# A two-layer hybrid backbone step: first norm and first products in another order, output turned on TensorE, modulation pieces fetched two ahead

## The chip, the core and the metric

The kernel runs on one core of a Trainium2 chip. Its engines are TensorE (PE, which has a separate row for its weight loads, PEld), VectorE (DVE), ScalarE (ACT), GpSimd (POOL) and SyncE (SP). DMAs are issued by SP, ACT or POOL. The metric is the device time of one execution in microseconds; a smaller number is better. Times of runs are medians. A profile is of one execution.

## The reference

One inference step for 128 context tokens and 256 latent tokens (384 in all), model width 1024, two layers:

```python
def trunk_layer(x, cvec, lp, mix_fn):
    sh1, sc1, gt1, sh2, sc2, gt2 = adaln(cvec, lp)       # silu(c) @ w_mod + b_mod, 6 x 1024
    h = modulate(rms_norm(x, lp["norm1_g"]), sh1, sc1)   # h * (1 + scale) + shift
    qa, ka, va, u, qc, kc, vc, g = project_inputs(h, lp) # h @ w_in, q and k normed
    oa, ob, oc, aux = mix_fn(qa, ka, va, u, qc, kc, vc)  # attention, S5 scan, neighbourhood attention
    x = x + gt1[:, None, :] * merge_branches(oa, ob, oc, g, lp)
    h2 = modulate(rms_norm(x, lp["norm2_g"]), sh2, sc2)
    x = x + gt2[:, None, :] * swiglu(h2, lp)
    return x, aux
```

with `rms_norm(x, g) = x * rsqrt(mean(x*x) + 1e-6) * g`. Context tokens are modulated by `c_ctx`, latent tokens by `c`. Behind the second layer stands one more `rms_norm` with `final_g`; that is the output `y`. All is float32.

## The kernel before, in words

Activations lie transposed: `xT` holds 8 tiles of 128 features by 384 tokens. A product in float32 precision is made of three float32r matmuls: high times high, high times low, low times high. `wsplit` (line 126) loads a 512 KB weight piece through SP (`raw`), ACT casts it to the high part `hi` (line 134) and DVE subtracts for the low part `lo` (line 136). The hidden state has the same two parts, `hh` and `hl` (`shift`, line 345): ACT writes `hh`, DVE `hl`, each in two instructions, one per token group.

PE's order is the order in which the program is written. The other engines' instructions are ordered by a scheduler with priorities (`high_priority`); `issue_after` puts an instruction behind another one in that order. Every engine takes its queue in order, so an instruction that waits holds up what stands behind it.

The start of layer 0 is `first` (line 473). 28 matmuls with a zero operand (`warm`) come first. ACT squares the 8 tiles of `xT` (line 482), DVE adds them into two sums (line 484), PE sums these over features (line 325, 3 token blocks by 2 buffers), DVE takes the reciprocal root in a chain of small operations (`rsqrt`, lines 145 to 161). `mod_col` (line 421) multiplies a 1 MB piece of `w_mod` with the conditioning vector, for one tile's shift and scale together: 8 matmuls, shown in the profile as 16 records; ACT copies the result (line 434); `mod_row` (line 437) turns it into columns on PE and DVE adds the bias. `norm_bc` (line 329) broadcasts the root over partitions on PE. `first_h` scales a tile (line 455) and calls `shift`. Then, for tile d from 0 to 7, `tok_mms` (line 459) issues nine matmuls for column block 1 and nine for block 0 (line 466); between them stand the `mod_col` of tile d+2, and behind them its `mod_row`, so that PE takes the modulation in turn with the products.

`s5_lambda` prepares the constants of the S5 scan: about 90 operations on DVE of 128x32 and a little more, a sine and a cosine on ACT (lines 632 and 633), which need another activation table. Before the change, all up to its first `yield` is issued ahead of `first`, and the rest behind the products of tile 0; its results are first used by the preparation steps (`next(prep)`) behind tile 1.

Later sections of the modulation of layer 0, and of layer 1, are made in pieces of 512 KB each (`modvec`, line 222), which are taken one by one between products (`mod_steps`); each piece was loaded when its matmuls were issued to the program, with a high priority.

The end is `final` (line 1339). ACT has already scaled each tile of `xT` by its gain (`xg`, line 1335) as the last residuals come out of the feed-forward network, and `norm_sum` (line 309) has squared it and added it to one sum. PE sums over features, DVE takes the root, PE broadcasts it, DVE multiplies `xg` by it in three instructions and SP sends out each part as `yT`, still transposed.

Of the kernel before, what the change touches and what calls it, by code (L numbers as in the profile page):

```python
# [19 lines left out]
L = 2  # L20
# [21 lines left out]
N_EARLY = (11, 11)  # L42
SECTIONS = (1, 0, 2, 3, 4, 5)
# [21 lines left out]
class Net:  # L65
    def __init__(self, ctx, tc, a, o):
# [12 lines left out]
        self.mod_pending = None  # L79
        self.mrp = None  # L80
# [45 lines left out]
    def wsplit(self, src, n=1024, after=None):  # L126
# [4 lines left out]
        with self.tc.high_priority(offset=30), \  # L131
# [4 lines left out]
            nc.vector.tensor_tensor(lo[:, :n], raw[:, :n], hi.bitcast(F32)[:, :n], op=OP.subtract)  # L136
# [8 lines left out]
    def rsqrt(self, src, n, scale, eps):  # L145
        v = self.nc.vector
        x, g, w = [self.small.tile([128, 32], F32, name=f"rs_{q}", bufs=1)[:, :n] for q in "xgw"]
        yi = self.small.tile([128, 32], I32, name="rs_i")[:, :n]
        h = self.small.tile([128, 32], F32, name="rs_r")[:, :n]
        v.tensor_scalar(x, src, scale, eps, op0=OP.mult, op1=OP.add)  # L150
# [70 lines left out]

    def modvec(self, l, s, raws=None):
# [86 lines left out]
    def norm_sum(self, k):  # L309
# [4 lines left out]
        else:  # L314
            sq = self.tmp.tile([128, T], F32, name="tp")
            nc.scalar.activation(sq, self.xT[:, k, :], AF.Square)
            self.sum_last = nc.vector.tensor_tensor(self.ssq, self.ssq, sq, op=OP.add)

    def norm_rs(self):
        nc = self.nc  # L320
        ps = self.pt.tile([128, 512], F32, name="pt")
        sums = self.ssq if isinstance(self.ssq, list) else [self.ssq]
        for t in range(3):
            for i, sq in enumerate(sums):
                nc.tensor.matmul(ps[:, t:t + 1], lhsT=sq[:, t * 128:(t + 1) * 128], rhs=self.ones,
                                 start=i == 0, stop=i == len(sums) - 1)
        return self.rsqrt(ps[:, 0:3], 3, 1.0 / D, EPS)
# [93 lines left out]
    def mod_col(self, d):  # L421
        nc = self.nc
        ps = self.pt.tile([128, 512], F32, name="pt")
        with self.tc.high_priority(offset=2000):
            raw = self.qkv[:, 2048 * (d % 2):2048 * (d % 2) + 2048]
            nc.sync.dma_start(raw, self.a["wmods"][d])
# [41 lines left out]

    def load_early(self):
# [3 lines left out]
    def first(self, prep, lam):  # L473
# [1117 lines left out]
```

## Time and profile before

| | |
|---|---|
| median of 3 runs | 1273.38 us (1269.96 to 1277.38) |
| profiled execution, its own time | 1272.04 us |
| span of its trace | 1270.3 us |
| PE busy | 1235.8 us (97%) |
| PE weight loads | 1125.8 us (89%) |
| DVE busy | 884.2 us (70%) |
| ACT busy | 568.5 us (45%) |
| POOL busy | 31.0 us (2%) |
| mean DMA rate | 150 GB/s |
| mean granted TensorE clock | 0.989 |

The span is a little shorter than the execution's own time. Busy shares are means over stages with different limits, so what a change in one stage is worth is read from that stage's chain: which wait ends last there. PE is busy nearly all the time, and matmuls overlap one another in the trace: a record's duration is longer than the distance to the next one. The granted clock of TensorE has two levels, full (1.00, 2.4 GHz) and half (0.50, 1.2 GHz).

### The profile page before, as it was taken

What the parts mean: (1) busy time and instruction counts of PE and PEld (TensorE: products, weight loads), DVE (VectorE), ACT (ScalarE), POOL (GpSimd) and SP (SyncE); (2) the same over time, 40 slices, a digit from 0 to 9 for tenths busy, and PEclk for the clock granted to TensorE, in tenths of its full rate; (3) what the DMA queues carried; (4) which work ended last, traced back from release to release, by engine and by line L of the source; (5) the groups of instructions that cost most, each with busy time, mean ns of one, the idle gap of its engine ahead of it and who ended that gap; (6) DMA issues with size and microseconds to landing.
All of it is one profiled execution on the core that took longest, in us unless ns stands there. A gap on an engine that the chain in (4) does not pass through costs nothing.

```text
span 1270.3 us, 19705 instructions
## 1 busy us (share of the span) xinstructions
PE 1235.8 (97%) x7676; PEld 1125.8 (89%) x7676; DVE 884.2 (70%) x1799; ACT 568.5 (45%) x1121; POOL 31.0 (2%) x57
## 2 busy tenths in 40 slices
PE   9999999999999999999999999999999999999996
PEld 5768797887988999999997899878799999999996
DVE  7895678667778976857869886674786554555554
ACT  4373237565443433433445533755644532333442
POOL 0000000000000100000000000000000000000000
PEclk8999999999999999999999999989999999999998
DMA  8856744223656744545473332332133434334331
GB/s 313 311 198 200 249 152 132 85 78 137 209 169 217 262 160 158 174 143 170 135 269 91 121 127 93 115 105 95 56 111 106 133 117 133 119 118 133 129 102 64
DMA packets 53581, 190.16 MB, mean 150 GB/s; under 512 B 7008, under 2 KB 7056, under 8 KB 52336
## 3 DMA queue, kind: packets, MB, share of 16 engines
q1 hardware_dynamic: 46368, 167.82, 40.1%
q0 software_dynamic: 4672, 16.30, 4.0%
q10 hardware_dynamic: 2448, 4.79, 1.1%
q8 instruction: 60, 0.98, 0.3%
q14 instruction: 33, 0.27, 0.1%
HBM read 186.49 MB, written 2.39 MB: 149 GB/s over the span
## 4 chain that ended last, share of the span: by engine, by line
PE 86%; ACT 6%; DVE 4%; DMA 2%; issue 1%; SPq 0%; DVEq 0%; ACTq 0%
PE ps L141 11%; PE ps L143 11%; PE pm L141 11%; PE ps L142 11%; PE pm L142 11%; PE pm L143 11%; PE ps L466 6%; PE pm L466 3%; PE ps L236 2%; DVE lo L136 2%; ACT hi L134 1%; PE ps L1066 1%; PE ps L836 1%; PE pt L915 1%; PE pt L1132 1%; PE pt L1106 1%
## 5 line engine op out<-in xcount | busy, mean ns | idle before, releaser
L136 DVE TENSOR_TENSOR lo<-raw,hi 128x1024 fp32r<-128x1024 f32 (+1 forms) x246 | 295.1, 1200 | 174.3 <-ACT hi L134 172.9
L134 ACT CAST hi<-raw 128x1024 fp32r<-128x1024 f32 (+1 forms) x246 | 253.2, 1032 | 310.1 <-PE pm L142 108.8
L141 PE MATMUL pm<-hh,hi 128*128 128x384 f32 x550 | 191.8, 349 | 0.0
L143 PE MATMUL pm<-hh,lo 128*128 128x384 f32 x550 | 185.7, 338 | 0.0
L142 PE MATMUL pm<-hl,hi 128*128 128x384 f32 x550 | 185.4, 337 | 0.0
L143 PE MATMUL ps<-ah,lo 128*128 128x386 f32 (+1 forms) x512 | 174.1, 340 | 1.5 <-DVE lo L136 1.4
L141 PE MATMUL ps<-ah,hi 128*128 128x386 f32 (+1 forms) x512 | 174.9, 342 | 0.0
L142 PE MATMUL ps<-al,hi 128*128 128x386 f32 (+1 forms) x512 | 173.4, 339 | 0.0
L141 PEld LDWEIGHTS pm<-hh,hi 128*128 128x128 f32 x550 | 104.5, 190 | 12.9 <-issue 9.1
L141 PE MATMUL pm<-ah,hi 128*128 128x386 f32 (+1 forms) x320 | 113.1, 353 | 0.0
L143 PE MATMUL pm<-ah,lo 128*128 128x386 f32 (+1 forms) x320 | 109.1, 341 | 2.4 <-DVE lo L136 2.4
L142 PE MATMUL pm<-al,hi 128*128 128x386 f32 (+1 forms) x320 | 109.1, 341 | 0.0
L141 PE MATMUL ps<-hh,hi 128*128 128x384 f32 x314 | 105.7, 337 | 0.0
L143 PE MATMUL ps<-hh,lo 128*128 128x384 f32 x314 | 104.9, 334 | 0.0
L142 PE MATMUL ps<-hl,hi 128*128 128x384 f32 x314 | 104.9, 334 | 0.0
L142 PEld LDWEIGHTS pm<-hl,hi 128*128 128x128 f32 x550 | 104.7, 190 | 0.0
L143 PEld LDWEIGHTS pm<-hh,lo 128*128 128x128 f32 x550 | 104.2, 190 | 0.0
L143 PEld LDWEIGHTS ps<-ah,lo 128*128 128x128 f32 x512 | 96.6, 189 | 2.8 <-DVE lo L136 2.8
L141 PEld LDWEIGHTS ps<-ah,hi 128*128 128x128 f32 x512 | 96.3, 188 | 3.0 <-issue 1.9
L142 PEld LDWEIGHTS ps<-al,hi 128*128 128x128 f32 x512 | 96.8, 189 | 0.0
L141 PEld LDWEIGHTS pm<-ah,hi 128*128 128x128 f32 x320 | 60.6, 190 | 8.5 <-issue 3.4
L1224 DVE SCALAR_TENSOR_TENSOR xT<-ps,mod,xT 128x128 f32<-128x128 f32 x84 | 31.2, 412 | 51.9 <-PE ps L143 51.9
(318 smaller groups left out, 2072.1 us busy)
## 6 DMA issues: line engine op xcount, KB each, us to landing
raw<-wgu SPq DMA_DIRECT2D x88, 512.0 KB, 3.5
raw<-wg SPq DMA_DIRECT2D x48, 512.0 KB, 3.5
raw<-wq SPq DMA_DIRECT2D x28, 512.0 KB, 4.1
raw<-wd SPq DMA_DIRECT2D x32, 448.0 KB, 3.4
qkv<-wmodt POOLq DMA_DIRECT2D x24, 512.0 KB, 4.2
mr<-wmod SPq DMA_DIRECT2D x22, 512.0 KB, 4.6
qkv<-wmods SPq DMA_DIRECT2D x8, 1024.0 KB, 5.8
raw<-wo SPq DMA_DIRECT2D x16, 512.0 KB, 3.5
```

Of the source, the lines that this page charges most:

```text
L134: nc.scalar.copy(hi[:, :n], raw[:, :n])
L136: nc.vector.tensor_tensor(lo[:, :n], raw[:, :n], hi.bitcast(F32)[:, :n], op=OP.subtract)
L141: mm(ps, lhsT=wh, rhs=xh, start=start, stop=False)
L142: mm(ps, lhsT=wh, rhs=xl, start=False, stop=False)
L143: mm(ps, lhsT=wl, rhs=xh, start=False, stop=stop)
L236: nc.tensor.matmul(ps[32 * q:32 * q + cs.shape[-1], 0:256], lhsT=cs, rhs=raw[:, q * 256:(q + 1) * 256], start=k % 4 == 0, stop=k % 4 == 3)
L466: self.nc.tensor.matmul(ps[t][:, :w], lhsT=h[:, k, ts], rhs=x[:, c:c + w], start=k == 0 and i == 0, stop=k == KT - 1 and i == 2)
L836: nc.tensor.matmul(b[:, i, 0:NCOL], lhsT=G[:, 8 * d + 4 * h + i, r, :], rhs=u4[:, 4 * h + i, :], start=True, stop=True)
L915: mm(y, lhsT=E[:, 8 * d + p, r].rearrange("p a b -> p (a b)"), rhs=H[d][r][:, i, d:d + NCOL], start=False, stop=d == 1 and r == 1)
L1066: nc.tensor.matmul(u["S"][:, i, :], lhsT=Q[hb, h // 2, t * 128:(t + 1) * 128], rhs=K[hb, ks, k0:k0 + n], start=True, stop=True)
L1106: nc.tensor.transpose(pp[:, i, :], f[:, i * 128:(i + 1) * 128], self.ident)
L1224: self.res_last = self.nc.vector.scalar_tensor_tensor(self.xT[:, m, c0:c1], ps[:, c0:c1], gt[:, m, g:g + 1], self.xT[:, m, c0:c1], op0=OP. ...
```

## The change

It edits four places.

1. In `first`, the warm block has 16 matmuls instead of 28, and the block ahead of the first products 3 instead of 4. The squares go to eight buffers; tiles 5 and 7 are squared on DVE, the others on ACT. DVE adds tiles 1, 2 and 3 into tile 0; PE sums five buffers. `xT` is loaded by SP and ACT in turn, and `cT` by POOL. Tile 0 is scaled with the broadcast straight from PSUM. The first nine products are grouped by their operands. The first part of `s5_lambda` is issued behind the reciprocal root.
2. In `modvec`, pieces of layer 0 are fetched two ahead.
3. `rope` is loaded behind an output on POOL's queue, and the pieces of `mod_col` behind the weight piece last issued.
4. In `final`, PE turns `xg` back to tokens by features in 24 transposes; the last square is summed on PE without DVE's add; the root multiplies the turned tiles per token, half on ACT, half on DVE. The output `y` goes out in four DMAs.

```diff
+N_WARM = (16, 3, 3)
...
-    def rsqrt(self, src, n, scale, eps):
+    def rsqrt(self, src, scale, eps):
...
+        c = n // len(src)
+        for i, q in enumerate(src):
+            v.tensor_scalar(x[:, c * i:c * i + c], q, scale, eps, op0=OP.mult, op1=OP.add)
...
-            nc.sync.dma_start(self.cT.rearrange("p k g -> p (k g)"), a["cT"])
             self.xT = c.tile([128, KT, T], F32, name="xT")
             for k in range(0, KT, 2):
-                nc.sync.dma_start(self.xT[:, k:k + 2].rearrange("p k t -> p (k t)"),
-                                  a["xT"][:, k * T:(k + 2) * T])
+                (nc.scalar if k % 4 else nc.sync).dma_start(
+                    self.xT[:, k:k + 2].rearrange("p k t -> p (k t)"),
+                    a["xT"][:, k * T:(k + 2) * T])
+            nc.gpsimd.dma_start(self.cT.rearrange("p k g -> p (k g)"), a["cT"])
...
+    def mod_fetch(self, n):
+        while self.mod_list and len(self.mod_raws) < n:
+            self.mod_raws.append(self.mod_get(*self.mod_list.pop(0)))
...
-                with self.tc.high_priority(offset=2000):
-                    raw = self.mod_raw(l)
-                    with self.tc.issue_after(self.weights.ins):
-                        nc.sync.dma_start(raw, self.a["wmod"][l, s, k])
+                if l == 0:
+                    self.mod_fetch(2)
+                raw = self.mod_raws.pop(0) if self.mod_raws else self.mod_get(l, s, k)
...
+    def tok_first(self, ps, hi, lo):
+        for i, (h, x) in enumerate(((self.hh, hi), (self.hh, lo), (self.hl, hi))):
+            for t in range(3):
+                self.nc.tensor.matmul(ps[t], lhsT=h[:, 0, t * 128:(t + 1) * 128], rhs=x[:, 0:512],
+                                      start=i == 0, stop=False)
...
-        self.warm(28)
+        self.warm(N_WARM[0])
         with self.tc.high_priority(offset=1000):
-            self.ssq = [self.at(O_UD + T * i, T) for i in range(2)]
+            sq = self.at(O_G, KT, T)
             for k in range(KT):
...
+                x = self.xT[:, k]
+                if k in (5, 7):
+                    with self.tc.issue_after(add.ins):
+                        nc.vector.tensor_tensor(sq[:, k], x, x, op=OP.mult)
+                else:
+                    nc.scalar.activation(sq[:, k], x, AF.Square)
+                if k in (1, 2, 3):
+                    add = nc.vector.tensor_tensor(sq[:, 0], sq[:, 0], sq[:, k], op=OP.add)
+            self.ssq = [sq[:, k] for k in (0, 4, 5, 6, 7)]
             r = self.norm_rs()
             c = self.mod_col(0)
-            self.warm(3)
+        w = {(1, 0): self.wsplit(self.a["wq"][0, 4], after=self.rs_last)}
+        with self.tc.high_priority(offset=1000):
+            self.warm(N_WARM[1])
             am = self.mod_row(0, *c)
             pb = self.norm_bc(r)
...
+        with self.tc.high_priority(offset=900):
+            self.first_h(0, am, pb)
             bc = self.tmp.tile([128, T], F32, name="ssq", bufs=1)
             nc.scalar.copy(bc, pb[:, :T])
...
+        with self.tc.issue_after(self.rs_last.ins):
+            next(lam)
         c = self.mod_col(1)
-        self.warm(4)
+        self.warm(N_WARM[2])
...
             if d == 0:
-                self.tok_mms(ps[1], 0, *w[1, 0], 0, 512)
+                self.tok_first(ps[1], *w[1, 0])
...
     def final(self):
         nc = self.nc
-        r = self.norm_rs()
-        self.warm(7)
-        bc = self.norm_bc(r)
-        for k0, k1 in ((0, 3), (3, 6), (6, 8)):
-            n = k1 - k0
-            nc.vector.tensor_tensor(self.xg[:, k0:k1], self.xg[:, k0:k1],
-                                    bc[:, None, :T].to_broadcast([128, n, T]), op=OP.mult)
-            nc.sync.dma_start(self.o["yT"][:, k0:k1], self.xg[:, k0:k1])
+        ps = [self.acc() for _ in range(6)]
+        for k in range(KT):
+            if k == KT - 2:
+                r = self.norm_rs()
+            for t in range(3):
+                nc.tensor.transpose(ps[3 * (k // 4) + t][:, 128 * (k % 4):128 * (k % 4) + 128],
+                                    self.xg[:, k, 128 * t:128 * t + 128], self.ident)
+        y = self.at(KT * T, 3, 2, 512)
+        for t in range(3):
+            nc.scalar.activation(y[:, t, 0], ps[t], AF.Copy, scale=r[:, t:t + 1])
+            nc.vector.tensor_scalar(y[:, t, 1], ps[3 + t], r[:, t:t + 1], None, op0=OP.mult)
+            o = self.o["y"][:, t].rearrange("p (h c) -> p h c", h=2)
+            if t < 2:
+                nc.sync.dma_start(o, y[:, t])
+            else:
+                nc.scalar.dma_start(o[:, 0], y[:, t, 0])
+                nc.sync.dma_start(o[:, 1], y[:, t, 1])
...
-        next(lam)
```

How this moves instructions is seen in three places. Line numbers of the changed kernel differ from those of the kernel before; the names do not.

On ACT, from the high part of tile 0 (`hh`) to that of tile 2, in the kernel before; `arena<-pt` is the copy of a modulation column, `hi<-raw` the cast of a weight piece:

```order
L349 ACTIVATE hh<-tp,mod_114 128x256
L434 COPY arena<-pt 128x256
L134 CAST hi<-raw 128x1024 x2
L349 ACTIVATE hh<-tp,mod_114 128x128
L349 ACTIVATE hh<-tp,mod_114 128x256
L434 COPY arena<-pt 128x256
L349 ACTIVATE hh<-tp,mod_114 128x128
```

And in the changed kernel, where `ssq<-pt` is the copy of the broadcast and `sl_sn`, `sl_cn` are sine and cosine of `s5_lambda`:

```order
L374 ACTIVATE hh<-tp,mod_114 128x256
L533 COPY ssq<-pt 128x384
L460 COPY arena<-pt 128x256
L137 CAST hi<-raw 128x1024
L374 ACTIVATE hh<-tp,mod_114 128x128
L374 ACTIVATE hh<-tp,mod_114 128x256
L672 ACT_TABLE_LOAD
L672 ACTIVATE sl_sn<-sl_r 128x32
L673 ACTIVATE sl_cn<-sl_r_246 128x32
L460 COPY arena<-pt 128x256
L137 CAST hi<-raw 128x1024
L374 ACTIVATE hh<-tp,mod_114 128x128
```

The table load, the sine and the cosine have moved from ahead of the first column copy to between the high part of tile 1 and the column copy of tile 2, and one cast stands ahead of tile 0 now.

On PE, the sums and what follows them, in the kernel before; `ones` are the sums, `cs` the modulation columns:

```order
L325 MATMUL pt<-ones,arena 128x1 x6
L431 MATMUL pt<-qkv,cs_123 32x256 x4
L431 MATMUL pt<-qkv,cs 2x256 x4
L167 LDWEIGHTS zero
L167 MATMUL pt<-zero 128x512
```

And in the changed kernel:

```order
L350 MATMUL ps<-ones,arena 128x1 x15
L457 MATMUL pt<-qkv,cs_123 32x256 x4
L457 MATMUL pt<-qkv,cs 2x256 x4
L173 LDWEIGHTS zero
L173 MATMUL pt<-zero 128x512
```

There are nine more summing matmuls; what stands behind them is the same.

On PE at the end of the program, in the kernel before, from the last products on:

```order
L142 MATMUL ps<-hl,hi 128x384
L143 MATMUL ps<-hh,lo 128x384
L325 MATMUL pt<-ones,ssq 128x1 x3
L167 LDWEIGHTS zero
L167 MATMUL pt<-zero 128x512
```

And in the changed kernel, where `ident` marks a transpose and `tp` holds the last square:

```order
L1386 MATMUL ps<-ident,arena 128x128 x12
L1386 MATMUL pm<-ident,arena 128x128 x2
L1386 MATMUL ps<-ident,arena 128x128
L1386 MATMUL pm<-ident,arena 128x128 x2
L1386 MATMUL ps<-ident,arena 128x128
L350 MATMUL pt<-ones,ssq 128x1
L350 MATMUL pt<-ones,tp 128x1
```

18 transposes stand ahead of the sums, which are six instead of three; six more transposes stand behind them, and the zero matmuls and the broadcast are gone.

## Rows read from the trace of the kernel before

**Rows 1.** Chain that ended last, head: start us, us, what it was on

```profile
10.50 1.28 PE pt L325 x10
11.78 1.00 PE pt L431 x16
...
13.94 0.88 PE pt L440 x4
14.82 1.50 PE pt L332 x6
...
23.13 0.34 PE pt L440 x4
```

**Rows 2.** Windows of one microsecond in the head: engines' busy time, then PEclk, DMA

```profile
12.00:13.00 1.00, 1.00 (x18) 0.33 (x11) 1.00 (x13) 0.00 (x0) 0.00 (x0) 0.99 0.98 406
13.00:14.00 1.00, 1.00 (x4) 0.23 (x3) 1.00 (x13) 0.72 (x3) 0.00 (x0) 0.50 1.01 392
```

**Rows 3.** Timeline of the head: start us, us, engine, line, what, count, [idle before]

```profile
1.17 8.67 PE L167 MATMUL pt<-zero 128*128 128x512 bf16 x28 [1.17 <-DVE zero L189]
...
1.24 0.69 POOL L181 DMA_DIRECT2D ident<-ident  x1 [0.79 <-POOLq L1583]
...
4.23 0.64 DVE L599 SCALAR_TENSOR_TENSOR ee_q<-ee_q,ee_x 128x32 f32<-128x32 f32 x3
...
6.09 1.99 ACT L482 ACTIVATE tp<-xT 128x384 f32<-128x384 f32 x4 [0.23 <-DMA xT<-xT]
...
6.22 3.12 PEld L167 LDWEIGHTS <-zero 128*128 128x128 bf16 x15 [0.23 <-issue]
...
9.82 1.28 ACT L632 ACT_TABLE_LOAD   x1
...
26.94 0.49 PE L466 MATMUL ps<-hi,hh 128*128 128x512 f32 x1
...
32.76 0.47 PE L466 MATMUL ps<-hi,hh 128*128 128x512 f32 x1
```

**Rows 4.** DMA issues by line: size and median us from issue to landing

```profile
yT<-arena SPq DMA_DIRECT2D x1, 384.0 KB, 3.1
...
ident<-ident POOLq DMA_DIRECT2D x1, 64.0 KB, 3.8
...
cT<-cT SPq DMA_DIRECT2D x1, 8.0 KB, 1.8
```

**Rows 5.** Waits of PE from 60 to 130 us: total, times, longest

```profile
PE ps L236 <- DMA mr<-wmod: 1.0, 1, 1.0
```

**Rows 6.** Chain that ended last, tail

```profile
1255.45 0.19 PE ps L143
...
1257.67 0.83 PE pt L325 x6
```

**Rows 7.** Timeline of the tail

```profile
1258.53 0.16 DVE L150 TENSOR_SCALAR rs_x<-pt 128x3 f32<-128x3 f32 x1 [0.92 <-PE pt L325]
...
1260.45 0.16 DVE L157 SCALAR_TENSOR_TENSOR rs_r<-rs_w,rs_r 128x3 f32<-128x3 f32 x1
...
1262.41 3.48 DVE L1346 TENSOR_TENSOR arena<-arena,pt 128x1152 f32<-128x1152 f32 x3 [1.80 <-PE pt L332]
1263.84 2.41 SPq L1348 DMA_DIRECT2D yT<-arena  x3
```

**Rows 8.** Window of one microsecond in the tail

```profile
1258.00:1259.00 1.00, 1.00 (x8) 0.65 (x8) 0.40 (x3) 0.00 (x0) 0.00 (x0) 0.93 0.00 0
```

**Rows 9.** Timeline of DVE, tile 1 of the first products

```profile
21.84 1.22 DVE L136 TENSOR_TENSOR lo<-raw,hi 128x1024 fp32r<-128x1024 f32 x1
...
24.05 0.74 DVE L455 SCALAR_TENSOR_TENSOR tp<-xT,am,ssq 128x128 f32<-128x128 f32 x2
...
25.37 0.49 DVE L352 SCALAR_TENSOR_TENSOR hl<-tp,mod,hh 128x256 fp32r<-128x256 f32 x1 [0.16 <-ACT hh L349]
```

**Rows 10.** Chain that ended last, four transposes

```profile
75.83 0.44 PE pt L575 x4
```

More of the change, by code (lines that the diff above doesn't have):

```diff
@@ L79, in __init__ @@
         self.mod_pending = None
+        self.mod_raws = []
+        self.mod_list = [(0, s, k) for s in SECTIONS[2:4] for k in range(KT)]
         self.mrp = None
@@ L143, in mm3 @@
         mm(ps, lhsT=wl, rhs=xh, start=False, stop=stop)
-    def rsqrt(self, src, n, scale, eps):
+    def rsqrt(self, src, scale, eps):
         v = self.nc.vector
+        n = sum(q.shape[-1] for q in src)
         x, g, w = [self.small.tile([128, 32], F32, name=f"rs_{q}", bufs=1)[:, :n] for q in "xgw"]
@@ L220, in mod_load, with mod_get @@
         return raw
+    def mod_get(self, l, s, k):
+        with self.tc.high_priority(offset=2000):
+            raw = self.mod_raw(l)
+            with self.tc.issue_after(self.weights.ins):
+                self.nc.sync.dma_start(raw, self.a["wmod"][l, s, k])
+        return raw
+    def mod_fetch(self, n):
+        while self.mod_list and len(self.mod_raws) < n:
+            self.mod_raws.append(self.mod_get(*self.mod_list.pop(0)))
     def modvec(self, l, s, raws=None):
@@ L307, in section, with norm_sum @@
         return self.mod[l][:, i * KT:(i + 1) * KT, :]
-    def norm_sum(self, k):
+    def norm_sum(self, k, last=False):
         nc = self.nc
@@ L316, in norm_sum @@
             nc.scalar.activation(sq, self.xT[:, k, :], AF.Square)
-            self.sum_last = nc.vector.tensor_tensor(self.ssq, self.ssq, sq, op=OP.add)
+            if last:
+                self.ssq = [self.ssq, sq]
+            else:
+                self.sum_last = nc.vector.tensor_tensor(self.ssq, self.ssq, sq, op=OP.add)
     def norm_rs(self):
         nc = self.nc
-        ps = self.pt.tile([128, 512], F32, name="pt")
         sums = self.ssq if isinstance(self.ssq, list) else [self.ssq]
[L323 to L327, printed above, removed]
+        if len(sums) > 2:
+            ps = [self.acc(t) for t in range(3)]
+            todo = [(t, i) for i in range(len(sums)) for t in range(3)]
+        else:
+            pt = self.pt.tile([128, 512], F32, name="pt")
+            ps = [pt[:, t:t + 1] for t in range(3)]
+            todo = [(t, i) for t in range(3) for i in range(len(sums))]
+        for t, i in todo:
+            nc.tensor.matmul(ps[t][:, 0:1], lhsT=sums[i][:, t * 128:(t + 1) * 128], rhs=self.ones,
+                             start=i == 0, stop=i == len(sums) - 1)
+        return self.rsqrt([p[:, 0:1] for p in ps] if len(sums) > 2 else [pt[:, 0:3]], 1.0 / D, EPS)
     def norm_bc(self, r):
@@ L425, in mod_col @@
             raw = self.qkv[:, 2048 * (d % 2):2048 * (d % 2) + 2048]
-            nc.sync.dma_start(raw, self.a["wmods"][d])
+            with self.tc.issue_after(self.weights.ins) if d else ExitStack():
+                nc.sync.dma_start(raw, self.a["wmods"][d])
         raw = raw.rearrange("p (k c) -> p k c", k=KT)
@@ L557, in project_tok @@
             self.evac(n, ps)
-        nc.gpsimd.dma_start(self.o["ga_v"][l], self.v[:, 0, 0:128])
+        self.rope_after = nc.gpsimd.dma_start(self.o["ga_v"][l], self.v[:, 0, 0:128])
         nc.gpsimd.dma_start(self.o["na_v"][l], self.v[:, 0, 128:384])
@@ L999, in att_prep @@
             v.tensor_reduce(ss[:, t * 10:(t + 1) * 10], sq, axis=AX.X, op=OP.add)
-        r = self.rsqrt(ss, 30, 1.0 / HD, EPS)
+        r = self.rsqrt([ss], 1.0 / HD, EPS)
         tt = lambda d, x, y, op: v.tensor_tensor(d, x, y, op=op)
@@ L1331, in ffn @@
                         with self.tc.high_priority(offset=120):
-                            self.norm_sum(q[0])
+                            self.norm_sum(q[0], l == L - 1 and q[0] == KT - 1)
                             if l:
@@ L1340, in final @@
         nc = self.nc
-        r = self.norm_rs()
-        self.warm(7)
-        bc = self.norm_bc(r)
-        for k0, k1 in ((0, 3), (3, 6), (6, 8)):
-            n = k1 - k0
-            nc.vector.tensor_tensor(self.xg[:, k0:k1], self.xg[:, k0:k1],
-                                    bc[:, None, :T].to_broadcast([128, n, T]), op=OP.mult)
-            nc.sync.dma_start(self.o["yT"][:, k0:k1], self.xg[:, k0:k1])
+        ps = [self.acc() for _ in range(6)]
[12 more added lines that the diff above has]
+                nc.sync.dma_start(o, y[:, t])
+            else:
+                nc.scalar.dma_start(o[:, 0], y[:, t, 0])
+                nc.sync.dma_start(o[:, 1], y[:, t, 1])
     def dyn(self, name):
@@ L1430, in body @@
                 self.rope = self.const.tile([128, 2, 2, HD], F32, name="rope")
-                self.nc.gpsimd.dma_start(self.rope.rearrange("p a t d -> p (a t d)"), self.a["rope"])
+                with self.tc.issue_after(self.rope_after.ins):
+                    self.nc.gpsimd.dma_start(self.rope.rearrange("p a t d -> p (a t d)"),
+                                             self.a["rope"])
             with self.dyn(f"s5_{l}") as p:
@@ L1465, in build @@
         Net(ctx, tc, a, o).run()
[L1468 removed]
+OUTS = dict(y=[128, 3, D], ga_k=[L, 128, 128], ga_v=[L, 128, 128], na_k=[L, 128, 256],
             na_v=[L, 128, 256], ssm=[L, 128, 32])
@@ L1572, in unlayout @@
 def unlayout(r):
-    y = r["yT"].transpose(2, 1, 0).reshape(T, D)
+    y = r["y"].transpose(1, 0, 2).reshape(T, D)
     ssm = r["ssm"].reshape(L, 2, 64, 2, 2, 8).transpose(0, 4, 3, 5, 1, 2).reshape(1, L, 2, 2, 16, 64)
```

14 lines of the change are left out of this document (3 added, 11 removed).

## The prediction, on record before the changed kernel ran

> **What bounds the kernel now.** I read the chain of waits first, then the same stretches of the timeline, then the granted clock by microsecond. From about 21 us on TensorE sets the pace: between the products of tile 0 and those of tile 2 nothing is late, and the reader is to see in the chain that product, modulation and product follow without a hole [rows 1, 3]. All that can be won lies before those products and behind the last one, because the change touches little else. At the front the chain runs through the sums of squares (ending 11.78), the modulation columns of tile 0, three zero matmuls, the modulation row and the broadcast, which ends at 14.82 + 1.50 = 16.32; the first nine products end at 23.13 [rows 1]. The granted clock goes from full (2.4 GHz) to half (1.2 GHz) at 13.0, after PE had done zero matmuls until 9.84 and then only light work; it is why two pairs of a modulation row take 0.88 us at 13.94 and 0.34 at 23.13 [rows 1 to 3]. At the back the last product ends at 1255.64 and the span 14.7 us later [rows 6]; in between stand sums, rsqrt, a broadcast, three DVE products and three output transfers [rows 6 to 8].
>
> **Step 1, the sums.** The squares go to one buffer each, DVE adds only tiles 1 to 3 into tile 0, and PE sums five buffers: 15 matmuls, where there were 6. Six were 12 records, and ten of those took 1.28 us, 0.128 each [rows 1]; 15 are 30 records. When do they start? `cT` moves to POOL's queue, and the tanh stands ahead of the squares on ACT. On SP a small piece landed 1.8 us after issue, on POOL the first transfer, 64 KB, took 3.8 [rows 4]; it was issued at 1.24 [rows 3], so `cT` lands between 3.0 and 5.0. I take 5.0, the POOL row. Tanh then ends at 5.2, four squares at 0.5 (four took 1.99) at 7.2 [rows 3], the third add at 7.75. From there 30 records at full clock end at 11.6. At half clock a record is 0.88/4 = 0.22 to 1.50/6 = 0.25 [rows 1], and 30 of 0.235 end at 14.8. Between these: the warm block has 16 instead of 28 matmuls. Of the 28, 15 ran in the last 3.12 us and 13 in the 5.05 before [rows 3], so 16 end at about 6.9, 2.9 us earlier than 9.84. If the clock falls earlier by as much, at 10.1, 18 records run at full clock and 12 at 0.235, and the sums end at 12.9: 1.1 later than now (bounds -0.2 and +3.0). The transfers of `x` start earlier, on two queues, but the sums are held by PE, not by the last tile.
>
> **Step 2, sums to broadcast.** Now 4.54 us, partly at each clock. After: 16 modulation records, three zero matmuls, the row, the broadcast. At full clock 1.0 (as at 11.78) + 0.64 (three at 3.12/15) + 0.34 (as at 23.13) + 0.77 (half of 1.50) = 2.75, at half twice that, 5.5 [rows 1, 3]. The rsqrt sets a floor: 1258.53 to 1260.61 in the tail, 2.08, plus two more single-column reads, some 0.3, plus 0.77 of broadcast, 3.15 [rows 7]. I take the middle of 3.15 and 5.5, 4.35: -0.2. The broadcast then ends at 17.25, +0.9.
>
> **Step 3, broadcast to the products of tile 2.** Now 32.76 - 16.32 = 16.4, and tile 1 starts at 26.94, 10.6 behind the broadcast [rows 1, 3]. Gone are the copy of the broadcast ahead of tile 0 and the wait of the products for the low part of the weights; products are grouped so that the low parts are wanted later. If nothing else were late, PE alone would need 13.6 us from the broadcast to tile 2 at full clock: columns 1.0, three zero matmuls 0.64, a row 0.34 and twice the 5.82 us that lie between the starts of tiles 1 and 2 (18 products, one column group and one row); or 15.2 with columns and zero matmuls at half.
> But the lambda chain (75 small DVE operations), which ran under the transfers, the squares and the rsqrt, now starts behind the rsqrt and shares DVE with the first tiles. What is queued behind it counts on ACT: table load, sine and cosine now stand between the high part of tile 1 and the copy of the modulation column of tile 2, and PE wants that copy before the products of tile 1. Counted from the broadcast's end: scaling and low part of tile 0 end at 2.0; seven operations that wait for one another at 0.21 (three took 0.64), 1.5; seven more, 1.0; the weights' low part 1.2; modulation, gain and four small ones 0.8; scaling of tile 1 0.74; 7.2. Its low part ends 1.07 behind (25.86 to 24.79 now), at 8.3; eight lambda operations in two chains that alternate, 0.105 each, at 9.1; sine and cosine 0.5, copy 0.35, row 0.34: products of tile 1 at 10.3, 0.3 earlier than now [rows 1, 3, 9]. In the same way tile 2, from the cosine at 9.6: 30 operations more (3.6), modulation, gain, five small ones and scaling 1.4, high part 0.6, a weight cast of 1.0 that stands ahead of the copy, copy and row 0.7: 16.9, against 16.4 now, +0.5. Later tiles have slack on DVE. Bounds -2.8 (PE alone) and +1.5 (75 operations at 0.02 more each).
> The table load itself took 1.28 us and stood in a hole of ACT [rows 3]; now it lies beside DVE's eight operations and costs nothing in this sum. The Trainium skill (ScalarE: Activation LUTs, What ACT_TABLE_LOAD costs) adds a drain of about 1.38 us to each switch, which no row here shows: by it the copy would be about 1.3 us later and the head +2.7 in place of +1.4. I go by the row.
> Sum of the head: 0.9 + 0.5 = **+1.4 us** (bounds -0.2 - 1.4 - 2.8 = -4.4 and 3.0 + 1.0 + 1.5 = +5.5).
>
> **Step 4, the modulation pieces.** In SP's queue only one 512 KB piece moves ahead of one weight piece; behind it the order is as it was. It waits for no buffer, and the weight piece behind it waits for DVE anyway. PE waited 1.0 us for such a piece once [rows 5], later than the moved one. I take 0, bounds -1.0 and +0.4 (one issue). The `rope` table goes behind an output on POOL, long before use: 0.
>
> **Step 5, the tail.** 18 transposes follow the last product at 0.11 (four took 0.44) [rows 10], to 1257.65; their banks are free. The sums then have two buffers, 12 records, against 6 in 0.83 that began at 1257.67 [rows 6]. At 0.128 they end at 1259.2; with the clock's fall inside 1258 to 1259 [rows 8] at 1259.5, against 1258.5: what the omitted add gives is eaten here. Rsqrt 2.1: 1261.65. Then three stages of ACT and DVE side by side, 512 elements each; DVE's 3072 elements took 3.48 us [rows 7], so 0.6 a stage, to 1263.45, against 1265.89. Broadcast and warm block are gone. The output DMAs start at 1262.3 in place of 1263.84 and the last 2.45 us earlier. The last landed 3.1 us after its issue [rows 4]; four transfers of the same 1.57 MB in a shorter time will queue, so of 2.45 I take **-1.5** (the first issue's lead), bounds -2.4 and -0.2 (sums wholly at half clock).
>
> **Sum.** 1272.04 + 1.4 + 0 - 1.5 = 1271.94 against the profiled execution's 1272.04. That execution lies 1.34 below the median of the runs, 1273.38, so I forecast 1273.38 - 0.1 = **1273.3 us**: no change that can be told.
>
> **Rivals.**
> A, the head gains as its order suggests: sums at full clock (11.6), broadcast at 15.0, lambda chain never in PE's way, tile 2 at 15.0 + 15.2 = 30.2 against 32.76, -2.6; tail -1.5. It needs the clock to hold until 11.6. For it: DVE waited at the modulation rows, so it has room. Against it: fewer zero matmuls ahead. Time 1273.38 - 2.6 - 1.5 = 1269.3; with all best bounds (4.4, 1.0 and 2.4) 1265.6.
> B, slower: the clock falls before or at the first sums, since PE has only the light sums between 6.9 and the columns. Place: 7.75 to the first products. Price: sums +3.0, the stretch to the broadcast +1.0, and the lambda chain's +0.5, with the tail at -0.4: 1273.38 + 4.1 = 1277.5. It decides once fewer than about five records run at full clock. For it: the fall at 13.0 came when PE was busy in the same light way [rows 2]. Against: the first groups of sums start within a microsecond of the warm block.
> C, the change in the loads does more than the order shows: PE's wait of 1.0 us goes and the weights come sooner, 1273.3 - 1.0 = 1272.3.
>
> **Numbers.** Forecast 0.53, A 0.27, B 0.15, C 0.05. A measurement tells about 0.5%, 6.4 us, from no change: below 1267.0 lies only the better end of A, 0.12; above 1279.75 only B with every step past its worst bound, 0.05; within, 0.83. The range from 1267 to 1278.5 takes in A and B at their own prices and about half of the way from A's price to its best bounds; the forecast's own is 1271 to 1276.
>
> **What would show it.** Sums: the last sum's record near 12.9, 30 records, and the granted clock half before 13.0. Lambda chain: ACT's column copy of tile 2 behind sine and cosine, PE waiting about a microsecond on it. Tail: rsqrt starting near 1259.5 less or plus the head's shift, first output issue 1.5 us nearer to the last product. The forecast is wrong if tile 2's products start below 31 or above 35, or if the stretch from the last product to the end is not 12.4 to 14.5 us.

## The result and the profile after

The changed kernel takes 1278.63 us (median of 17 runs, 1276.08 to 1282.34) against 1272.06 for the kernel before (17 runs, 1267.51 to 1277.38). The ratio is 1.0053, with a 95% interval of 1.0043 to 1.0064: slower by 6.6 us, where 1273.3 and no change were forecast. The time lies just outside the stated range, and the sign is that of rival B.

The marks of the prediction in the two profiled executions (us):

| | before | after | later by |
|---|---|---|---|
| sums begin (the first product with `ones`) | 10.03 | 13.10 | 3.1 |
| sums end | 11.78 | 19.66 | 7.9 |
| broadcast ends | 16.32 | 25.05 | 8.7 |
| products of tile 2 begin | 32.76 | 42.02 | 9.3 |
| last product ends | 1255.64 | 1261.53 | 5.9 |
| end of the span | 1270.3 | 1274.3 | 4.0 |

The head loses 9.3 us, the tail gives back 1.9. Between them the profiled execution of before lost more time than the other: between 60 and 1250 us its granted clock was at half for 13.6 us (near 226, from 399 to 402 and from 833 to 840), that of the changed kernel for 6.8. So the middle is better compared with an execution that has the old head and fewer such stretches (the new end alone, below, 10.2 us at half): against it the changed kernel is 8.3 later at 60 us and 7.75 later at the last product. A head of 8.3 to 9.3, a middle near -0.6 and a tail of -1.9 give 5.8 to 6.8; the runs measure 6.6. The -0.6 need not be the change's: the two executions also differ by 3.4 us at half clock.

Where the head goes is seen in the chain of waits of the changed kernel (start, us, what), which answers to [rows 1]:

```profile
1.67 9.09 DMA s5lam<-s5lam
10.76 0.02 issue
10.78 0.04 DVE sl_t L653
10.81 0.07 issue
10.89 0.18 DVE cs L208
...
11.25 0.48 DVE arena L520
...
12.48 0.57 DVE arena L520
13.05 0.04 issue
13.10 6.56 PE ps L350 x30
19.66 1.86 PE pt L457 x16
21.52 1.39 PE pt L173 x3
22.91 0.65 PE pt L466 x4
23.56 1.49 PE pt L357 x6
```

It does not begin with the load of `xT` but with the 48 KB of `s5lam`, 9.1 us from issue to landing, and then with one DVE product that reads it. The timeline of DVE shows what stands around this product:

```profile
6.84 0.17 DVE L206 TENSOR_SCALAR ct<-ct 128x16 f32<-128x16 f32 x1 [5.66 <-ACT ct L205]
10.78 0.19 DVE L653 TENSOR_TENSOR sl_t<-s5lam 128x32 f32<-128x32 f32 x1 [3.77 <-DMA s5lam<-s5lam]
10.89 0.17 DVE L208 TENSOR_TENSOR cs<-ct,cT 128x16 f32<-128x16 f32 x1
11.09 0.16 DVE L211 COPY cs<-cs 128x10 f32<-128x10 f32 x1
11.17 1.87 DVE L520 TENSOR_TENSOR arena<-arena 128x384 f32<-128x384 f32 x3
```

The number in brackets is the idle time ahead of an instruction, with what ended it. DVE stood still for 3.77 us in front of a product of 0.19 us. Behind it wait the conditioning vector and the three adds, whose squares ACT had finished; ACT's squares ended at 9.28:

```profile
6.59 0.22 ACT L205 ACTIVATE ct<-cT 128x16 f32<-128x16 f32 x1 [3.15 <-DMA cT<-cT]
6.71 2.57 ACT L518 ACTIVATE arena<-xT 128x384 f32<-128x384 f32 x6
```

TensorE was meanwhile idle for 6.95 us. The windows of one microsecond (busy time of PE, PEld, DVE, ACT, POOL, then the granted clock, DMA share and GB/s) show what that did, against [rows 2]:

```profile
9.00:10.00 1.00, 0.00 (x0) 0.00 (x0) 0.00 (x0) 0.28 (x1) 0.00 (x0) 1.00 0.93 352
10.00:11.00 1.00, 0.00 (x0) 0.00 (x0) 0.22 (x2) 0.00 (x0) 0.00 (x0) 0.89 1.10 435
11.00:12.00 1.00, 0.00 (x0) 0.00 (x0) 0.86 (x4) 0.26 (x1) 0.00 (x0) 0.50 1.03 426
...
27.00:28.00 1.00, 1.00 (x4) 0.45 (x3) 0.86 (x7) 1.00 (x2) 0.00 (x0) 0.58 0.40 57
```

The clock fell to half (1.2 GHz) at about 10.8, after TensorE had done nothing since 6.15 and 2.3 us ahead of the sums, and was full again at about 27.8. So all 30 records of the sums took 0.219 each, and the columns, zero matmuls, row and broadcast behind them took nearly twice their full-clock figures.

Why was a product of the lambda chain ahead of the sums at all, when the first part of the chain is issued behind the root? It belongs to the second part (`mul(t2, li, li)`), which has no such condition. It reads nothing but `s5lam`, so the scheduler was free to place it, and placed it seventh on DVE. The order of the changed kernel's DVE shows it plainly, and the prediction overlooked it:

```
L206 TENSOR_SCALAR ct<-ct 128x16
L653 TENSOR_TENSOR sl_t_250<-s5lam 128x32
L208 TENSOR_TENSOR cs<-ct,cT 128x16
L211 COPY cs_123<-cs 128x5x2
L520 TENSOR_TENSOR arena<-arena 128x384
```

The kernel before has the same product as early, although the second part of the chain is written behind tile 0. There it cost nothing, because `s5lam` was there at 2.77:

```profile
2.77 0.23 DVE L591 TENSOR_SCALAR ee_x<-s5lam 128x32 f32<-128x32 f32 x1 [1.59 <-DMA s5lam<-s5lam]
2.86 0.18 DVE L613 TENSOR_TENSOR sl_t<-s5lam 128x32 f32<-128x32 f32 x1
```

So both the early place and the operand were to be seen before the change ran; what was new is the transfer's place behind `xT`.

The Trainium skill (PSUM — Partial Sum Buffer, Engine vs sequencer instructions) says that the queues of VectorE, ScalarE and GpSimdE are strictly first in, first out. The 3.77 us agree: nothing behind the product ran while it waited.

### The profile page after: what moved, and what is told of

Read it like the earlier page. It is cut to its first block, busy times and chain, and to the rows that moved or that the text cites. A ratio compares the mean times of both kernels' runs of the same rounds, so it can differ in the third digit from the quotient of the medians.

```text
span 1274.3 us, 19757 instructions
## 1 busy us (share of the span) xinstructions
PE 1233.7 (97%) x7698; PEld 1127.6 (88%) x7698; DVE 881.8 (69%) x1799; ACT 569.0 (45%) x1122; POOL 31.6 (2%) x58
## 4 chain that ended last, share of the span: by engine, by line
PE 85%; ACT 6%; DVE 6%; DMA 2%; issue 1%; DVEq 0%; ACTq 0%
PE ps L144 11%; PE ps L146 11%; PE ps L145 11%; PE pm L144 11%; PE pm L145 10%; PE pm L146 10%; PE ps L492 5%; PE pm L492 3%; PE ps L253 2%; DVE lo L139 2%; ACT hi L137 2%; PE ps L876 1%; PE pt L955 1%; PE ps L1106 1%; PE pt L1172 1%
## 5 line engine op out<-in xcount | busy, mean ns | idle before, releaser
L144 PEld LDWEIGHTS pm<-hh,hi 128*128 128x128 f32 x550 | 103.8, 189 | 12.3 <-issue 8.6
```

The lines of the kernel that those rows point to most:

```text
L144: mm(ps, lhsT=wh, rhs=xh, start=start, stop=False)
```

## Experiments

Theory H: DVE's queue is held by the product that waits for `s5lam`. Rivals: the shorter warm block and its clock (C), the late loads (L), the number of summing matmuls (N). A last group asks for the parts that are left. All ratios are to the kernel before, with 95% intervals; each kernel is described by what it changes.

**One product behind the root.**

```diff
-        mul(t2, li, li)
+        with self.tc.issue_after(self.rs_last.ins):
+            mul(t2, li, li)
```

> The changed kernel with one DVE product of the lambda chain (sl_t<-s5lam, 0.19 us) put behind the reciprocal root with the rest of the chain. Theory H (held queue): this product stands in DVE's queue ahead of the first adds and waits for s5lam until 10.78 us, so the adds start at 11.25 and the sums at 13.10. Then here the adds follow their squares, the third ends near 9.0, sums begin near 9.0 and end between 13.0 (full clock, 0.128 each) and 15.6 (half, 0.22), against 19.66; products of tile 2 at 35 to 38 against 42.0; time 1272 to 1275 against 1278.6. Theory C (clock): what costs is the half clock after the shorter warm block; the sums begin earlier, but all of the head stays at half clock and the sums end at 15.6. Theory L (loads): the adds are late because cT and xT land late; then the sums begin at 13 as before and nothing is won.

Measured: 1273.85, ratio 1.0021 (1.0006 to 1.0036). The chain of waits now begins with `cT`:

```profile
1.25 5.62 DMA cT<-cT
6.87 0.02 issue
6.89 0.22 ACT ct L205
7.10 0.83 ACT arena L518 x2
7.94 0.02 issue
7.96 0.57 DVE arena L520
```

and the sums on PE follow the third add:

```profile
9.90 6.48 PE L350 MATMUL ps<-ones,arena 128*128 128x1 f32 x30 [2.44 <-DVE arena L520]
```

DVE's wait of 3.8 us is gone, the sums begin at 9.90 in place of 13.10 and tile 2 at 37.76 in place of 42.02. One condition on one instruction takes back 0.32 of the 0.53%, some 4 us. H is shown for that part. What is left looks like C: the clock falls at 10.0 and the sums still run at half clock, to 16.4. The warm block is tried together with this condition below.

**`s5lam` issued first.** The transfer goes ahead of `xT` on ACT's queue; the product stays where it is.

> The changed kernel with the transfer of s5lam issued first on ACT's queue, ahead of the two pieces of xT; the product that reads it stays ahead of the adds. Theory H with a late transfer as its cause: s5lam lands 2 to 4 us after its issue instead of 9.1, the product is done before the tanh, and the sums begin within 0.7 us of the other kernel's (product behind the root), near 9.0 to 9.6; the pieces of xT on ACT move by one issue, 0.45. If the position on the queue is not what made the transfer late, it lands near 10 again and the sums begin at 13.

Measured: 1273.77, ratio 1.0023 (1.0004 to 1.0042). `s5lam` lands 4.2 us after its issue, the product runs at 4.95, and the sums begin at 10.28, 0.4 behind those of the kernel above. Mending the transfer or the order gives the same time, so it was the meeting of the two: a product placed early, and its operand behind two pieces of 384 KB on one queue.

**28 zero matmuls again.** `N_WARM` is (28, 3, 4), nothing else.

> The changed kernel with the warm block of the kernel before, 28 + 3 + 4 zero matmuls instead of 16 + 3 + 3; the lambda product stays where it is. Theory H: the sums still begin at 13.1; the warm block ends at 9.8, PE is idle for 3.3 us, the clock falls at some point in the sums or before, and the gain is 0 to 3 us. Theory C: the clock is still full at 13.1 and for most of the sums; they end near 17.0 instead of 19.66, the columns, zero matmuls, row and broadcast behind them take 2.75 in place of 5.5, and tile 2 begins 4 to 5 us earlier; time near 1274.

Measured: 1277.5, ratio 1.0047 (1.0031 to 1.0064). The warm block ends at 8.8, the sums begin at 13.54 and take 6.56 us, as at (16, 3, 3). C alone falls: zero matmuls that end 4.7 us ahead of the sums do not keep the clock. Where tile 2 stood at 42.0, it stands at 42.8.

**The new end alone.** The kernel before, with the new `final`.

> The kernel before with the new end alone: output turned on TensorE, last square summed on PE, root applied per token, four output transfers. The head, the loads and the modulation are those of before. The profiles of the two kernels put the stretch from the last product to the end of the span at 14.67 and 12.77, so all theories expect 1.9 us less than the kernel before, 1270.2 against 1272.1, and first products at the times of before. If the transposes or the four transfers have a price elsewhere, it is less than 1.9.

Measured: 1269.27, ratio 0.9978 (0.9960 to 0.9995), 1.8 below the kernel before run beside it, 1271.07. The tail is a gain, so the loss lies in what this kernel lacks, the head and the loads; the profiles put it in the head (8.3 us at 60 us, 7.75 at the last product).

**Product behind the root, and 28 zero matmuls.**

> The changed kernel with the lambda product behind the root and the warm block of before (28, 3, 4). With the product alone behind the root the sums began at 9.90, 2.4 us behind the last zero matmul, and all 30 records ran at half clock (6.48 us). Theory C2 (what is left of the loss is the clock, since TensorE is idle between the warm block and the sums): here the zero matmuls last until 8.8 to 9.8, the sums begin at 9.9, run at 0.128 a record and end near 13.8 instead of 16.3; columns, zero matmuls, row and broadcast follow partly at full clock; products of tile 2 near 34 instead of 37.8; time near 1271, that of the kernel before. Theory N (nine more summing matmuls cost by their number, whatever is ahead of them): the clock falls at the sums all the same, they end near 16, and time stays at 1273.8.

**Product behind the root, and `cT` first on SP.**

> The changed kernel with the lambda product behind the root and cT again issued first on SP (16 zero matmuls as changed). In the changed kernel cT landed at 6.5 and the first square began at 6.7, against 4.9 before. Theory L2 (the late cT delays the squares by 1.8): cT lands near 2.5 to 3, squares run as their pieces of xT land, sums begin 1 to 2.4 us earlier than 9.9, near 8, TensorE is idle for less than 2 us, and more of the sums runs at full clock; they end between 12 (full) and 14.6 (half). If xT itself is what holds the squares, they begin at 6.5 or later and nothing is won.

**All three.**

> Both: lambda product behind the root, cT first on SP, 28 + 3 + 4 zero matmuls. The sums cannot begin before the zero matmuls end, 8.8 to 9.8; 30 records at 0.128 end at 12.7 to 13.7, against 11.78 in the kernel before. With the chain of small operations still behind the root the products of tile 2 begin near 33 to 34 (32.8 before), and with the new end's 1.9 the time is within 1.5 of the kernel before, 1270 to 1272.

Measured: 1272.58 (1.0013, 0.9998 to 1.0027), 1272.68 (1.0009, 0.9991 to 1.0027) and 1271.04 (0.9998, 0.9982 to 1.0013). With 28 zero matmuls PE is idle for 0.93 us ahead of the sums instead of 2.44; they begin at 10.07, the clock falls between 11 and 12, and they end at 15.3, between C2 and N. With `cT` on SP the tanh runs at 3.88 but the first square at 6.38, because its piece of `xT`, issued on SP behind `cT`, lands at 6.36 (at 4.90 in the kernel before); the sums begin at 9.29, and the clock falls between 11 and 12, within them. They end at 13.6, but tile 2 begins at 38.32, no earlier than with the product alone (37.76): the stretch from the broadcast to tile 2 takes 19.3 in place of 16.7, which was not followed. By time neither step can be told from the product alone, whose interval overlaps both. With both, PE goes from zero matmuls to sums without a pause:

```profile
1.17 8.48 PE L173 MATMUL pt<-zero 128*128 128x512 bf16 x28 [1.17 <-DVE zero L196]
9.48 3.54 PE L350 MATMUL ps<-ones,arena 128*128 128x1 f32 x30
12.95 1.93 PE L457 MATMUL pt<-qkv,cs 128*32 128x256 f32 x16
```

30 records take 3.5 us, 0.118 each, and end at 13.0. So nine more matmuls, 18 records, cost 2.1 us at full clock and, at 0.219 each, 3.9 at half.

That kernel reaches tile 2 at 33.74, level with the one that has the new end alone (33.73), but its tile 4 begins 3.3 later (48.61 against 45.35). Its DVE is held once more, by the first step of a preparation that waits for `s5c`, with tile 4's scaling behind it (the wait ends at 45.39):

```profile
40.08 0.23 DVE L473 TENSOR_SCALAR am<-mod,gains 128x2 f32<-128x2 f32 x1
45.39 0.29 DVE L785 TENSOR_SCALAR arena<-arena 128x256 f32<-128x256 f32 x1 [5.08 <-DMA arena<-s5c]
45.60 0.74 DVE L481 SCALAR_TENSOR_TENSOR tp<-xT,am,ssq 128x128 f32<-128x128 f32 x2
```

**The chain early too.** As the last kernel, with `s5lam` first on ACT and the first part of the lambda chain issued ahead of the sums, as before the change.

```diff
+        next(lam)
         self.mrp, self.mrn = p, 4
...
-        with self.tc.issue_after(self.rs_last.ins):
-            next(lam)
```

> As the kernel before this one (cT first on SP, 28 zero matmuls), and besides s5lam first on ACT and the first part of the lambda chain issued ahead of the sums, as in the kernel before the change. In the changed kernel PE waits 0.72 and 0.94 us for column copies that stand behind the sine and the cosine, and the stretch from the broadcast's end to the products of tile 2 is 17.0. Theory of the moved chain: both waits go, this stretch becomes 15.0 to 15.6, and the kernel is 1.5 us faster than the same one with the chain behind the root. If the chain costs as much between the adds and the root, the sums and the root come later by as much and the time stays.

Measured: 1267.63, ratio 0.9973 (0.9956 to 0.9990), 3.4 us below the kernel without it. PE's waits for the column copies are gone, and the stretch from the broadcast (18.14) to tile 2 (32.95) is 14.8 in place of 16.4. That is 1.6, as expected; but the broadcast itself ends 0.8 later, since the bias of the modulation row now stands ahead of the root's last operation and waits 1.29 us for the row, so that tile 2 begins only 0.8 earlier. The larger part is tile 4, which begins at 44.57, 4.0 earlier, since the same wait for `s5c` is 1.6 us and no longer 5.1. In the two profiled executions this lead is gone at the last product (1253.17 against 1253.22), where the one with the lead has 10.2 us at half clock between 60 and 1250 us and the other 3.4; the medians show it, with intervals that overlap slightly. The wait for `s5c` was 4.5 to 5.1 us in the three kernels with 28 zero matmuls and the chain behind the root, where `s5c` landed 8.0 to 8.5 us after its issue, and absent in the changed kernel and the three variants with 16 zero matmuls, where it landed after 2.9 to 3.0; what makes the difference was not tried.

**Two buffers.** From this kernel, the squares and adds of before.

> The kernel with the chain early, cT and s5lam first and 28 zero matmuls (1267.6 against 1271.3 for the kernel before), with the sums as before the change: all squares on ACT, DVE adds them into two buffers, PE sums two (6 matmuls, 12 records). Theory N (the nine more summing matmuls cost by their number): in the kernel it starts from 30 records take 3.40 us behind a warm block that ends at 9.86; 12 records at 0.13 to 0.15 take 1.7, so the sums end up to 1.6 earlier, at 11.5 to 12.4, and the time falls by 0.5 to 1.5. Against it: eight DVE operations at 0.56 that share DVE with the lambda chain end later than the last square, 10.0; if the sums begin at 10.6 or later, they end no earlier and the five buffers are worth what they cost.

Measured: 1271.09, ratio 1.0000 (0.9983 to 1.0017): 3.5 us above the kernel it starts from (the two intervals overlap slightly), where N expected a gain. The sums end 0.8 earlier (12.3), but the order of DVE changed with them: the bias of the modulation row now stands in the middle of the root's chain, four of its operations behind it in place of one, and waits 1.2 us, until the row from PE ends. The granted clock, at half from about 13 in both, is full again at 19.7 in place of 16.4, so row and broadcast run at half. The broadcast ends no sooner, 18.23, and tile 2 begins 1.0 later; the rest of the difference lies behind the head and was not followed. N is not borne out; what the five buffers are worth by themselves stays open, since the order and the clock differ too.

**The old loads.** From the same kernel, no fetching ahead.

> The kernel with the chain early, cT and s5lam first and 28 zero matmuls, with the modulation loads as before the change: no fetching two ahead and mod_col's pieces free on SP's queue. Prediction's step 4 (0, between -1.0 and +0.4): products of tile 2 within 0.5 of 32.95, and a time within 1 us of 1267.6. If fetching ahead is worth its wait, PE's wait for a piece near 75 or 130 us grows here by up to 1 us.

Measured: 1270.09, ratio 0.9985 (0.9966 to 1.0003). Tile 2 begins at 34.02, 1.1 later; the bias again stands in the root's chain and waits for the row. PE's wait for a modulation piece is 1.3 against 0.9, but among the kernels with the new loads it is anything from 0.8 to 1.8. Both expectations, tile 2 within 0.5 and the time within 1 us, were missed, and since the order of DVE changed too, the run is inconclusive on the loads.

**New end and first products.** The kernel before with the new end, the first nine products grouped, and tile 0 scaled from PSUM.

> The kernel before with the new end, and of the new head only the grouping of the first nine products by operands and tile 0 scaled straight from PSUM. With the new end alone PE waited 0.89 us for the low part of the weights behind the first product, and tile 1's products began at 27.93, tile 2's at 33.73. Expected: the wait goes or shrinks to 0.3, the first products begin at most 0.5 earlier (ACT's copy of the broadcast is no longer ahead of the scaling), and tile 2's products begin 0.5 to 1.4 earlier than 33.7; time 0.5 to 1.4 below 1269.3. If the weights' high or low part ends last, nothing is won but the wait moves.

Measured: 1268.02, ratio 0.9974 (0.9957 to 0.9991). The wait for the low part falls from 0.89 to 0.45, tile 2 begins at 33.22, 0.5 earlier, the low end of what was expected. By time it cannot be told from the new end alone, 0.9978: the intervals overlap almost wholly.

**No third block.** From the kernel with the chain early, without the four zero matmuls ahead of the products.

> The kernel with the chain early, cT and s5lam first and 28 zero matmuls (1267.6 against 1271.3 for the kernel before), without the third block of zero matmuls (4) ahead of the first products. In it that block waits 1.07 us for ACT's copy of the broadcast, because its bank is that of the broadcast, which tile 0's scaling now reads straight from PSUM; the products begin at 20.88, while their operands hh and the weights' high part are ready by 19.8 and hl by 20.4. Expected: PE goes from the columns of tile 1 (19.1) to the products at about 19.8, 1.0 earlier, tile 2 near 32, time 0.5 to 1.0 below that kernel's, 0.9965 of the kernel before. If the pause without the block lets the granted clock fall among the first products, nothing is won.

Measured: 1267.97, ratio 0.9973 (0.9961 to 0.9985). Tile 2 begins at 31.69, 1.3 earlier, and the clock stays full; in the two profiled executions 1.1 of it is still there at the last product (1252.10 against 1253.17). The medians do not show it; their intervals, 0.9961 to 0.9985 and 0.9956 to 0.9990, are too wide for 1.3 us.

## Why the prediction was wrong

**Step 1 failed**, at "the third add at 7.75". It ended at 13.05, because DVE waited for `s5lam`, a wait that the step put at nothing. Sums were to end at 12.9, within 11.6 and 14.8; they ended at 19.66, outside both bounds. With that, tile 2 began at 42.02, above the 35 that the prediction named as a sign of being wrong. Three things were wrong in the step:

- DVE was taken to be free. The product of the second part of the chain held it until 10.78 (H, shown by two experiments, some 4 us of the time). The prediction wrote of 75 operations behind the root and did not check each queue for an operation that comes early and waits for a transfer.
- `cT` was to land between 3.0 and 5.0. It landed at 6.6, 5.3 us after its issue: the 1.8 and 3.8 us of [rows 4] were measured in another order of transfers (the last section has its time beside and behind pieces of `xT`). `s5lam` went from 2.0 to 9.1. And with `cT` in time the first square would still have waited for its piece of `xT`, until 6.38 where the step has 5.2. The step's words that the sums "are held by PE, not by the last tile" then fail: in the kernel with the product moved the chain from `cT` over squares and adds holds the sums, until 9.90.
- The clock was to fall at 10.1, since the warm block ended 2.9 earlier. It fell at about 10.8, a fair guess, but with PE idle and not under the sums; and it met them from their first record on, and not two thirds through.

With product, `cT` and zero matmuls mended, the sums end at 13.0. That this is nearly the step's 12.9 is luck: the step has them begin at 7.75 and run into half clock, here they begin behind the last zero matmul at 9.6 and run at full clock throughout. With the 16 zero matmuls of the step and the other two mended, they run from 9.29 to 13.6.

**Step 2** (4.35, between 3.15 and 5.5) came out at 5.39, wholly at half clock: its upper end.

**Step 3** was right in size and mechanism: 16.97 from the broadcast to tile 2 against 16.9, 9.96 against 10.3 for tile 1. PE waits 0.72 and 0.94 us for the column copies:

```profile
34.55 0.61 PE L466 MATMUL pt<-sel,arena 128*128 128x2 f32 x4 [0.72 <-ACT arena L460]
41.56 0.61 PE L466 MATMUL pt<-sel,arena 128*128 128x2 f32 x4 [0.94 <-ACT arena L460]
```

One part differs: up to tile 1's row at 30.57 PE, at half clock, was the later by 0.3 us, and DVE from there on. With the product moved, the clock is full from 20.3, DVE holds the stretch from the broadcast on, and it is 16.7. This is ACT around the sine:

```profile
31.56 0.90 ACT L374 ACTIVATE hh<-tp,mod 128x128 fp32r<-128x128 f32 x2 [3.26 <-DVE tp L481]
32.48 1.28 ACT L672 ACT_TABLE_LOAD   x1
33.89 0.23 ACT L672 ACTIVATE sl_sn<-sl_r 128x32 f32<-128x32 f32 x1
34.02 0.21 ACT L673 ACTIVATE sl_cn<-sl_r 128x32 f32<-128x32 f32 x1
34.14 0.35 ACT L460 COPY arena<-pt 128x256 f32<-128x256 f32 x1
```

The load takes 1.28 us, starts right behind the high part of tile 1 and is followed within 0.13 us by the sine. The drain of 1.38 us that the Trainium skill adds to a switch (ScalarE: Activation LUTs, What ACT_TABLE_LOAD costs) has no room in these rows; the row was the better guide.

**Step 4** (0) cannot be told from 0: the middle of the changed kernel is 0.6 shorter than that of the kernel with the new end alone, with 3.4 us less at half clock, and the test of the loads was inconclusive. **Rival C** is not borne out: it has the wait of 1.0 us of [rows 5] go, and in the changed kernel it is 1.65:

```profile
140.86 0.61 PE L253 MATMUL ps<-mr,cs 128*2 128x256 f32 x8 [1.65 <-DMA mr<-wmod]
```

**Step 5** was right: -1.5 forecast, 12.77 against 14.67 measured, -1.9, and -1.8 with the new end alone. The last rows of the tail, which answer to [rows 7], are

```profile
1266.94 1.84 ACT L1390 ACTIVATE arena<-ps,rs_r 128x512 f32<-128x512 f32 x3 [3.51 <-DVE rs_r L163]
1266.96 1.41 DVE L1391 TENSOR_SCALAR arena<-pm,rs_r 128x512 f32<-128x512 f32 x2
1267.77 1.01 SPq L1394 DMA_DIRECT2D y<-arena  x2
1268.28 0.74 DVE L1391 TENSOR_SCALAR arena<-ps,rs_r 128x512 f32<-128x512 f32 x1
```

The three stages take 2.1 us against 1.8 forecast, and the first output is issued 6.2 behind the last product instead of 8.2. The 0.4 above the forecast comes from the sums: they end 3.2 behind the last product, where 3.9 was forecast with the clock's fall inside them, and the granted clock stayed full until 1266.9.

**Rival B** had the place (up to the broadcast) and, partly by luck, nearly the time (1277.5). Its 4.1 above the kernel before stand against 6.6 measured, and they are made of sums at +3.0 and a tail at -0.4, where the profiles have +7.9 and -1.9. It has the clock fall because fewer zero matmuls are run; giving them back alone changed 1278.6 to 1277.5. Against B the prediction set that "the first groups of sums start within a microsecond of the warm block"; they started 6.95 us behind it, because DVE was held. With the product moved, what remains is close to B: PE idle for 2.44 us, all sums at half clock, ending 4.6 later than in the kernel before. **Rival A** is near the mended kernel by its size, 3.7 below the kernel before against A's 4.1, but not by its path: about half of the 3.7 is the tail's 1.8, tile 2 begins at 32.95 and not at 30.2, and the chain, `cT` and the warm block are back where they were.

## What to carry to other kernels

When a chain of small operations is moved, go through the new order engine by engine and look for the first instruction on each queue whose operand comes from a transfer: one product of 0.19 us held DVE for 3.8 us and put the products of tile 2 back by 4.3. The operation that depended on nothing but a constant's load was the one that the scheduler placed early, so give such an operation the same condition as the rest of its chain. Do not take the landing time of a small transfer from a trace in which it went first; price it for the transfers that are issued ahead of it and beside it. And compare medians of several executions for the whole, but single marks for a stage: two profiled executions differed by several microseconds of half clock in the middle, whatever the head did.

## What the runs showed of the hardware that was not expected

Small transfers landed far later beside large ones. `cT`, 8 KB, took 1.7 to 1.9 us as the first on SP with only `s5lam` issued at the same time, 3.0 to 3.1 with a piece of `xT` issued at that time on ACT, and 5.3 to 6.0 on POOL, half a microsecond behind pieces of `xT` on both queues. `s5lam`, 48 KB, took 1.9 to 2.0 as the first on ACT with `cT` first on SP, 4.2 as the first on ACT with a piece of `xT` first on SP, and 9.1 to 10.1 behind two pieces of `xT`. Two queues did not bring the first piece of `xT` sooner (4.85 in the changed kernel, 4.90 before); the last landed at 8.05 in place of 8.84, having been issued at 1.19 in place of 2.60. The DMA issues of before (size, median us from issue to landing) have

```profile
xT<-xT SPq DMA_DIRECT2D x4, 384.0 KB, 4.7
```

and those of after

```profile
xT<-xT ACTq DMA_DIRECT2D x2, 384.0 KB, 5.6
xT<-xT SPq DMA_DIRECT2D x2, 384.0 KB, 5.0
```

With `cT` in time, the first square began at 5.8 to 6.4 on two queues, against 4.9 in the kernel before. The Trainium skill (DMA: Bandwidth & Descriptors, Issuing engines are not separate DMA queues) says that transfers interleave on the same 16 engines whichever engine starts them, and that several issuers save only the time of issuing. The medians agree: from issue to landing the pieces took no less, and the 1.4 us by which the last was issued earlier brought 0.8.

The granted clock also fell while TensorE was idle, in the changed kernel 4.6 us after its last zero matmul and in the one with 28 zero matmuls alone 2.1 us after it, and did not wait for light work to begin.
